# Softmax weights transposed by VectorE blocks and a round trip through DRAM instead of by TensorE

## The chip, the core and the metric

One core of one Trainium2 chip runs the whole program. The metric is device time in microseconds (us) of one execution. Five engines work side by side, each through its own instruction stream in order: PE (TensorE matmuls), DVE (VectorE), ACT (ScalarE), POOL (GpSimd) and SP (SyncE). POOL, SP and ACT also issue DMAs; an instruction that waits holds back what stands behind it on its engine. PEld is the loading of PE's weights, which runs beside the matmuls.

## What is computed

Two decoder layers on x of 512 rows by 1024 columns, all in float32. Layer 0 mixes tokens by dilated window attention, layer 1 by a gated linear recurrence (RG-LRU); after each comes a gated convolution FFN, and every sub-layer has a norm before and after it. Only the attention matters here. It has 24 heads of width 128 in three groups of 8, whose outputs are combined head by head with softmax denominators as weights:

```python
WINDOWS, DILATIONS = (128, 512, 2048), (1, 4, 16)
...
logits = einsum('bxhnqd,bxhnkd->bxhnqk', qs, kk) * scale + bias
logits = where(mask, logits, NEG_INF)
p = exp(logits - max(logits)); s = sum(p)
o = einsum('bxhnqk,bxhnkd->bxhnqd', p, vv) / s
...
alpha = softmax(stack(lses), axis=0)
o = sum(alpha[..., None] * stack(outs), axis=0)
```

The last product needs p with the keys on the partitions, while the softmax leaves it with the queries there. So every 128x128 block of p is transposed between the two products.

## The kernel before

**Large products.** Every weight matrix is loaded in pieces (`load`, L193, SP queue, three `raw` buffers), split into a high and a low float32r half (`split` L148 and `split_normed` L139: ACT makes `whi`, DVE makes `wlo`), and multiplied in three passes (`mm3`, L253, matmuls at L255; the value products at L643 and L702). At most eight split units wait in front of PE (`W_UNITS`).

**Order of work.** The program is written out by hand in one order. `feat_tiles` (L409) makes one output tile of 24 matmuls and calls `tick` (L222); `values` (L689) also ticks after each tile of 24 matmuls. A tick advances every side generator in `sides` whose delay has run out, and then `pump` (L167) converts one or two more weight units. A generator says with `yield n` after how many ticks it goes on. One tick is thus 24 matmuls of 512 columns.

**Local heads** (window 128, dilation 1). `local` (L744) runs once for each of 8 heads, two for each `hp`, one tick apart. Its first step loads a Toeplitz bias tile (`toeplitz`, L612, a DMA on POOL's queue), makes the scores on PE (L753, plain float32), adds the bias on DVE (L740) and takes the exponential on ACT (L766). Two ticks later it transposes the 7 blocks on PE (L775, into two PSUM banks), copied out by DVE (L780) and ACT (L778). One more tick later come the output products (L788) and their copy (L790).

**Strided heads** (dilations 4 and 16). `strided` (L793) takes the two groups of one head together, for 8 heads: Toeplitz tiles, scores (L803), bias (L740), exponentials (L818), normalising (L830). Two ticks later 8 transposes on PE (L837) and two copies on ACT (L839); then a row of coefficients goes through DRAM and comes back on all partitions (`crow` L842 and `cn` L844, POOL queue). Four ticks later (five for head 6) the output products (L850) and the combination on DVE (L853, L854).

**Blocks by DVE.** `turned` (L285) and `fetched` (L295) are already used by `prenorm` (L305) for one row tile of each of three norms: DVE turns each 32x32 block in itself (L288), one POOL DMA writes the tile to DRAM (L292), and four POOL DMAs of 32 partitions fetch it with the blocks in their places (L299). The tile that comes back is read through a strided view: 128 columns of one block are four runs of 32.

**Small vectors.** `feature_columns` (L524), a part of the generator `build`, loads biases and convolution weights as rows by POOL DMAs (L514), turns them on PE (L517) and copies them (L519); `ffn` and `lru` read them later.

**Buffers.** Nearly all 128x512 tiles come from one pool with 28 slots (`gen`, L118); a tile that takes a used slot waits for that slot's last reader. Toeplitz tiles have 2 slots, PSUM has 8 banks.

## Time and profile before

| | |
|---|---|
| Time, median of 3 runs | 1471.40 us (1471.37 to 1471.43) |
| The profiled execution's own time | 1471.48 us |
| Its span, first to last instruction | 1469.7 us |
| Granted TensorE clock | 0.998 |
| Busy share of PE, PEld, DVE, ACT, POOL | 99%, 84%, 58%, 46%, 4% |
| Transposes on PE at L775 and L837 | 56 and 64 |
| First score product of a local head, last output product of a strided one | 59.9 us, 481.9 us |

The profiled execution took 1471.48 us, of which 1.8 us lie outside its span. A PE row's duration is modelled and overlaps that of the next row, since matmuls are pipelined: what a matmul costs is read from the distance between starts.

### The profile page before, as it was taken

What the parts mean: (1) busy time and instruction counts of PE and PEld (TensorE: products, weight loads), DVE (VectorE), ACT (ScalarE), POOL (GpSimd) and SP (SyncE); (2) the same over time, 40 slices, a digit from 0 to 9 for tenths busy, and PEclk for the clock granted to TensorE, in tenths of its full rate; (3) what the DMA queues carried; (4) which work ended last, traced back from release to release, by engine and by line L of the source; (5) the groups of instructions that cost most, each with busy time, mean ns of one, the idle gap of its engine ahead of it and who ended that gap; (6) DMA issues with size and microseconds to landing.
All of it is one profiled execution on the core that took longest, in us unless ns stands there. A gap on an engine that the chain in (4) does not pass through costs nothing.

```text
span 1469.7 us, 18639 instructions
## 1 busy us (share of the span) xinstructions
PE 1461.2 (99%) x7006; PEld 1228.7 (84%) x7006; DVE 851.0 (58%) x1894; ACT 682.0 (46%) x1538; POOL 60.1 (4%) x141
## 2 busy tenths in 40 slices
PE   9999999999999999999999999999999999999998
PEld 7888888888888898888888888988898888888886
DVE  5645545454645786555564338868785555565333
ACT  7645536263625454433444234489554333444321
POOL 0500001010100100000000001000100000000000
PEclk9999999999999999999999999999999999999999
DMA  6622235343534433223233222441433223223201
GB/s 203 198 66 89 91 91 138 114 137 109 141 111 123 159 115 115 86 89 112 86 101 129 86 92 79 123 137 58 136 107 109 95 86 115 87 89 129 98 1 58
DMA packets 117331, 157.55 MB, mean 107 GB/s; under 512 B 5688, under 2 KB 98072, under 8 KB 117240
## 3 DMA queue, kind: packets, MB, share of 16 engines
q1 hardware_dynamic: 112104, 144.72, 30.1%
q0 software_dynamic: 4544, 10.58, 3.3%
q8 instruction: 55, 0.90, 0.3%
q10 hardware_dynamic: 592, 1.05, 0.2%
q14 instruction: 36, 0.29, 0.1%
HBM read 148.38 MB, written 7.95 MB: 106 GB/s over the span
## 4 chain that ended last, share of the span: by engine, by line
PE 93%; ACT 4%; DVE 3%; issue 0%; DVEq 0%; ACTq 0%
PE ps L255 55%; PE acc L255 24%; PE v L702 7%; PE v L643 2%; DVE xb L908 1%; PE O L850 1%; PE S L803 1%; PE O L788 1%; PE S L753 1%; DVE wlo L150 1%; ACT sig L929 1%; ACT whi L149 1%; PE tr L331 1%; PE PT L837 0%; PE PT L775 0%
## 5 line engine op out<-in xcount | busy, mean ns | idle before, releaser
L255 PE MATMUL ps<-hT,whi 128*128 128x512 f32 (+1 forms) x2752 | 801.8, 375 | 0.0
L255 PEld LDWEIGHTS ps<-hT,whi 128*128 128x128 f32 x2752 | 503.0, 188 | 91.4
L255 PE MATMUL ps<-hT,wlo 128*128 128x512 f32 (+1 forms) x1376 | 515.2, 374 | 0.0
L150 DVE TENSOR_TENSOR wlo<-raw,whi 128x512 fp32r<-128x512 f32 x360 | 230.9, 687 | 189.3 <-ACT whi L149 189.3
L255 PEld LDWEIGHTS ps<-hT,wlo 128*128 128x128 f32 x1376 | 259.0, 188 | 46.3
L149 ACT ACTIVATE whi<-raw 128x512 fp32r<-128x512 f32 x360 | 204.9, 623 | 135.2 <-PE acc L255 120.8
L567 DVE SCALAR_TENSOR_TENSOR u<-ps,cols,u 128x511 f32<-128x511 f32 x192 | 143.8, 749 | 140.6 <-ACT u L563 137.2
L255 PE MATMUL acc<-whi,ahi 128*128 128x512 f32 x512 | 199.6, 390 | 0.0
L255 PE MATMUL acc<-whi,alo 128*128 128x512 f32 x512 | 199.3, 389 | 0.2 <-DVE alo L150 0.2
L255 PE MATMUL acc<-wlo,ahi 128*128 128x512 f32 x512 | 199.2, 389 | 0.0
L143 ACT ACTIVATE whi<-raw,first_w 128x128 fp32r<-128x128 f32 (+1 forms) x432 | 147.2, 431 | 62.6 <-PE ps L255 52.9
L563 ACT ACTIVATE u<-ps,cols 128x512 f32<-128x512 f32 x96 | 75.0, 781 | 209.7 <-PE ps L255 209.7
L144 DVE SCALAR_TENSOR_TENSOR wlo<-raw,first_w,whi 128x128 fp32r<-128x128 f32 (+1 forms) x432 | 142.3, 394 | 37.4 <-ACT whi L143 37.3
L255 PEld LDWEIGHTS acc<-whi,alo 128*128 128x128 f32 x512 | 96.1, 188 | 20.6 <-DVE alo L150 0.6
L255 PEld LDWEIGHTS acc<-whi,ahi 128*128 128x128 f32 x512 | 96.1, 188 | 19.8
L255 PEld LDWEIGHTS acc<-wlo,ahi 128*128 128x128 f32 x512 | 96.1, 188 | 19.7
L702 PE MATMUL v<-whi,hT 128*128 128x512 f32 x320 | 103.6, 395 | 0.0
L702 PEld LDWEIGHTS v<-whi,hT 128*128 128x128 f32 x320 | 60.1, 188 | 12.1
L578 ACT ACTIVATE u<-u 128x512 f32<-128x512 f32 x48 | 30.4, 634 | 80.4 <-DVE u L567 80.4
L702 PE MATMUL v<-wlo,hT 128*128 128x512 f32 x160 | 62.3, 390 | 0.0
L382 DVE TENSOR_TENSOR post<-acc,gain 128x512 f32<-128x512 f32 x32 | 22.0, 687 | 45.3 <-ACT junk L262 45.3
L630 DVE TENSOR_TENSOR qk<-ps,roots 128x512 f32<-128x512 f32 x24 | 16.6, 691 | 53.3 <-PE ps L255 53.3
(168 smaller groups left out, 986.9 us busy)
## 6 DMA issues: line engine op xcount, KB each, us to landing
raw<-in_ffn_w_up_dram SPq DMA_DIRECT2D x48, 1024.0 KB, 5.2
raw<-in_attn_w_qkv_dram SPq DMA_DIRECT2D x26, 1024.0 KB, 5.1
raw<-in_ffn_w_down_dram SPq DMA_DIRECT2D x24, 1024.0 KB, 5.0
raw<-in_attn_w_qkv_dram SPq DMA_DIRECT2D x19, 512.0 KB, 6.3
raw<-in_lru_w_in_dram SPq DMA_DIRECT2D x8, 1024.0 KB, 5.4
vrows<-v SPq DMA_DIRECT2D x16, 256.0 KB, 3.8
vp<-vrows SPq DMA_DIRECT2D x16, 256.0 KB, 3.4
raw<-in_attn_w_o_dram SPq DMA_DIRECT2D x4, 1024.0 KB, 4.9
```

Of the source, the lines that this page charges most:

```text
L143: nc.scalar.activation(hi[:, k], raw[:, k], AF.Copy, scale=w)
L144: nc.vector.scalar_tensor_tensor(lo[:, k], raw[:, k], w, hi[:, k].bitcast(F32), op0=ALU.mult, op1=ALU.subtract)
L149: nc.scalar.activation(hi, raw, AF.Copy)
L150: nc.vector.tensor_tensor(lo, raw, hi.bitcast(F32), op=ALU.subtract)
L255: mm(dst, l[a], r[b], start=start and n == 0, stop=stop and n == 2)
L382: nc.vector.tensor_tensor(u[i], parts[i], g[:, at[i]], op=ALU.mult)
L563: nc.scalar.activation(u, ps, AF.Identity, scale=cc[:, j : j + 1], bias=cc[:, 48 + j : 49 + j])
L567: nc.vector.scalar_tensor_tensor(u[:, d:], ps[:, : S - d], wc, u[:, d:], op0=ALU.mult, op1=ALU.add)
L578: nc.scalar.activation(u, u, AF.Gelu_apprx_tanh)
L630: nc.vector.tensor_tensor(dst, src, row, op=ALU.mult)
L643: mm(banks[t], hT[a][:, k, t * P : (t + 1) * P], W[b][:, k % 2, :], start=u == n == 0, stop=u == 3 and n == 5,)
L702: mm(banks[t], hT[a][:, k, t * P : (t + 1) * P], W[b][:, k % 2, :], start=(k, a, b) == (0, 0, 0), stop=(k, a, b) == (KD - 1, 1, 0),)
```

## The change

Four things change.

- **Local heads**: all 8 turn p by `turned` and `fetched` in the first step, right behind the exponentials: a tile of 3 blocks and one of 4. The generator then yields 4 ticks where it yielded 2 and 1.
- **Strided heads**: heads 0 to 6 do the same behind the normalising, two tiles of 4 blocks, and yield 6 ticks (7 for head 6) where they yielded 2 and 4 (5). Head 7 keeps the transposes on PE. The DMA `crow` stands between the writes and the fetches, `cn` behind them.
- **Toeplitz tiles** are fetched one head ahead (`table`), and a strided head's two tiles lie in one buffer.
- **Rows of the small vectors** are loaded on the sync queue, in steps of the generator of their own (`column_rows`); their transposes follow in later steps.

The output products read the fetched tiles through the strided view. No head's arithmetic changes.

```diff
-    def turned(src, i):
-        T = gen(s="T")
+    def turned(src, n=4):
+        T = gen(s="T")[:, : n * P]
         nc.vector.transpose(
             T.rearrange("p (c n j) -> p c n j", c=4, j=32), src.rearrange("p (n c j) -> p c n j", c=4, j=32)
         )
-        d = dp.tile([P, 512], F32, name=nm("turned"))
+        d = dp.tile([P, n * P], F32, name=nm("turned"))
         nc.gpsimd.dma_start(d, T)
         return d
...
-    def columns(parts):
-        n = sum(c for _, c in parts)
+    def column_rows(parts):
         st = gen(s="st")
         at = 0
         for src, c in parts:
-            nc.gpsimd.dma_start(st[at : at + c, :P], src)
+            nc.sync.dma_start(st[at : at + c, :P], src)
             at += c
+        return st, at
+    def columns(st, n):
...
+        def table(strided, h, take=True):
+            if (strided, h) not in tables:
+                T = gp.tile([P, 256], F32, tag="toe", name=nm("toe"), bufs=TOE_BUFS)
+                for i in range(1 + strided):
+                    n = 256 >> strided
+                    toeplitz(T[:, i * n : i * n + n], i + strided, h, n)
+                tables[strided, h] = T
+            return tables.pop((strided, h)) if take else None
...
         def local(h, hh, q, k, v):
-            T = gp.tile([P, 256], F32, tag="toe", name=nm("toe"), bufs=TOE_BUFS)
-            toeplitz(T, 0, h, 256)
+            T = table(0, h)
...
-            yield 2
+            table(*((0, h + 1) if h < 7 else (1, 0)), False)
+            ds = [turned(L[0][:, P:], 3), turned(L[1])]
             blocks = [(a, j) for a in range(4) for j in range(2) if a or j]
-            pts = {}
-            for c in range(2):
-                grp = blocks[4 * c : 4 * c + 4]
-                ps = psum("PT")
-                for n, (a, j) in enumerate(grp):
-                    o = (a % 2) * 256 + j * P
-                    nc.tensor.transpose(ps[:, n * P : (n + 1) * P], L[a // 2][:, o : o + P], ident)
...
-            yield 1
+            pts = [fetched(ds[0], 3), fetched(ds[1])]
+            pts = {b: pts[n > 2][:, n - 3 * (n > 2)] for n, b in enumerate(blocks)}
+            yield 4
             po = psum("O")
...
-            yield 2
-            pts = []
-            for L in Ls:
-                ps = psum("PT")
-                for r in range(4):
-                    c = slice(r * P, (r + 1) * P)
-                    nc.tensor.transpose(ps[:, c], L[:, c], ident)
-                pt = gen(s="PT")
-                nc.scalar.activation(pt, ps, AF.Copy)
-                pts.append(pt)
+            if h < 7:
+                table(1, h + 1, False)
+                ds = [turned(L) for L in Ls]
             row = dp.tile([P, 4], F32, name=f"crow{h}")
             nc.gpsimd.dma_start(row, c0)
+            if h < 7:
+                pts = [fetched(d) for d in ds]
             cn = gen(s="cn")
             nc.gpsimd.dma_start(cn, bass.AP(tensor=row.tensor, offset=row.offset, ap=[[0, P], [1, S]]))
-            yield 5 if h == 6 else 4
+            if h < 7:
+                yield 7 if h == 6 else 6
+            else:
...
-                    mm(po[:, c], vtile(v, r, 2 * gi + hh), pts[gi][:, c], start=gi == 0, stop=gi == 1)
+                    mm(po[:, c], vtile(v, r, 2 * gi + hh), pts[gi][:, r], start=gi == 0, stop=gi == 1)
```

More of the change, by code (lines that the diff above doesn't have):

```diff
@@ L290, in turned, with fetched @@
         )
-        d = dp.tile([P, 512], F32, name=nm("turned"))
+        d = dp.tile([P, n * P], F32, name=nm("turned"))
         nc.gpsimd.dma_start(d, T)
         return d
-    def fetched(d):
-        t = gen(s="ft")
+    def fetched(d, n=4):
+        t = gen(s="ft")[:, : n * P]
         for c in range(4):
@@ L318, in prenorm @@
             return
-        ds = [turned(h, i) for i, h in enumerate(xs)]
+        ds = [turned(h) for h in xs]
         xt = [fetched(d) for d in ds]
@@ L526, in feature_columns @@
         v2 = lambda r: r.rearrange("n (j p) -> (n j) p", p=P)
-        cl = columns(
-            [(v(lru_conv_w[0, k]), 8) for k in range(4)]
-            + [(v(lru_conv_b[0]), 8), (v2(lru_ga_b[0]), 8), (v2(lru_gx_b[0]), 8), (v(lru_lambda[0]), 8)]
-        )
+        rows = [
+            column_rows(
+                [(v(lru_conv_w[0, k]), 8) for k in range(4)]
+                + [(v(lru_conv_b[0]), 8), (v2(lru_ga_b[0]), 8), (v2(lru_gx_b[0]), 8), (v(lru_lambda[0]), 8)]
+            )
+        ]
+        yield 1
+        for layer in range(2):
+            cw, cb = ffn_conv_w[layer], ffn_conv_b[layer]
+            rows.append(column_rows([(v(cw[0]), 48), (v(cw[1]), 48)]))
+            rows.append(column_rows([(v(cw[2]), 48), (v(cb), 48)]))
+            yield 1
+        cl = columns(*rows[0])
         lam = cl[:, 56:64]
@@ L550, in feature_columns @@
         for layer in range(2):
-            cw, cb = ffn_conv_w[layer], ffn_conv_b[layer]
-            ca = columns([(v(cw[0]), 48), (v(cw[1]), 48)])
-            cc = columns([(v(cw[2]), 48), (v(cb), 48)])
-            ffn_cols[layer] = (ca, cc)
+            ffn_cols[layer] = tuple(columns(*rows[1 + 2 * layer + i]) for i in range(2))
             yield 1
@@ L615, in toeplitz @@
             nc.gpsimd.dma_start(dst, bass.AP(tensor=rowv[g].tensor, offset=o, ap=[[1, P], [1, n]]))
+        tables = {}
+        def table(strided, h, take=True):
[6 more added lines that the diff above has]
+            return tables.pop((strided, h)) if take else None
         vrows = []
@@ L766, in local @@
                 nc.scalar.activation(ls, ls, AF.Exp, bias=neg[:, a : a + 1], accum_out=st0[:, a, 1, h : h + 1])
-            yield 2
+            table(*((0, h + 1) if h < 7 else (1, 0)), False)
+            ds = [turned(L[0][:, P:], 3), turned(L[1])]
             blocks = [(a, j) for a in range(4) for j in range(2) if a or j]
-            pts = {}
-            for c in range(2):
-                grp = blocks[4 * c : 4 * c + 4]
-                ps = psum("PT")
-                for n, (a, j) in enumerate(grp):
-                    o = (a % 2) * 256 + j * P
-                    nc.tensor.transpose(ps[:, n * P : (n + 1) * P], L[a // 2][:, o : o + P], ident)
-                pt = gen(s="PT")
-                if c:
-                    nc.scalar.activation(pt[:, : len(grp) * P], ps[:, : len(grp) * P], AF.Copy)
-                else:
-                    nc.vector.tensor_copy(pt, ps)
-                for n, b in enumerate(grp):
-                    pts[b] = pt[:, n * P : (n + 1) * P]
-            yield 1
+            pts = [fetched(ds[0], 3), fetched(ds[1])]
+            pts = {b: pts[n > 2][:, n - 3 * (n > 2)] for n, b in enumerate(blocks)}
+            yield 4
             po = psum("O")
@@ L796, in strided @@
             Ls = []
+            T = table(1, h)
             for gi, (q, k) in enumerate(qks):
-                T = gp.tile([P, 256], F32, tag="toe", name=nm("toe"), bufs=TOE_BUFS)
-                toeplitz(T[:, :P], gi + 1, h, P)
                 ps = psum("S")
@@ L806, in strided @@
                     c = slice(r * P, (r + 1) * P)
-                    scores(L[:, c], ps[:, c], T[:, :P], mx[:, 4 * gi + r : 4 * gi + r + 1])
+                    scores(L[:, c], ps[:, c], T[:, gi * P : gi * P + P], mx[:, 4 * gi + r : 4 * gi + r + 1])
                 Ls.append(L)
@@ L830, in strided @@
                 nc.vector.tensor_tensor(L3, L3, rden.unsqueeze(2).to_broadcast([P, 4, P]), op=ALU.mult)
-            yield 2
-            pts = []
-            for L in Ls:
-                ps = psum("PT")
-                for r in range(4):
-                    c = slice(r * P, (r + 1) * P)
-                    nc.tensor.transpose(ps[:, c], L[:, c], ident)
-                pt = gen(s="PT")
-                nc.scalar.activation(pt, ps, AF.Copy)
-                pts.append(pt)
+            if h < 7:
+                table(1, h + 1, False)
+                ds = [turned(L) for L in Ls]
             row = dp.tile([P, 4], F32, name=f"crow{h}")
             nc.gpsimd.dma_start(row, c0)
+            if h < 7:
+                pts = [fetched(d) for d in ds]
             cn = gen(s="cn")
             nc.gpsimd.dma_start(cn, bass.AP(tensor=row.tensor, offset=row.offset, ap=[[0, P], [1, S]]))
-            yield 5 if h == 6 else 4
+            if h < 7:
+                yield 7 if h == 6 else 6
+            else:
+                yield 2
+                pts = []
+                for L in Ls:
+                    ps = psum("PT")
+                    for r in range(4):
+                        c = slice(r * P, (r + 1) * P)
+                        nc.tensor.transpose(ps[:, c], L[:, c], ident)
+                    pt = gen(s="PT")
+                    nc.scalar.activation(pt, ps, AF.Copy)
+                    pts.append(pt.rearrange("p (r c) -> p r c", r=4))
+                yield 4
             po = psum("O")
```

## The prediction, made before the changed kernel had run

> **What bounds the kernel now.** First the page: the span, the engines, the chain that ended last. Then the waits of PE, and the two attention stages as windows (busy us and count of each engine, clock, DMA share).

> ```profile
> span 1469.7 us, 18639 instructions
> PE 1461.2 (99%) x7006; PEld 1228.7 (84%) x7006; DVE 851.0 (58%) x1894; ACT 682.0 (46%) x1538; POOL 60.1 (4%) x141
> PE 93%; ACT 4%; DVE 3%; issue 0%; DVEq 0%; ACTq 0%
> ```
> ```profile
> PE warm L1024 <- DVE one L1056: 1.5, 1, 1.5
> PE v L643 <- ACT hT L345: 0.2, 1, 0.2
> PE acc L255 <- DVE alo L150: 0.2, 1, 0.2
> ```
> ```profile
> 59.00:215.00 156.00, 156.00 (x784) 132.18 (x783) 85.67 (x290) 79.26 (x248) 5.64 (x10) 1.00 0.30 93
> 215.00:483.00 268.00, 268.00 (x1345) 227.26 (x1345) 142.12 (x480) 123.78 (x385) 16.15 (x30) 1.00 0.44 131
> ```

> PE carries 93% of the chain and waits 1.9 us in all, none of it in the attention. In the local stage (59 to 215) and the strided one (215 to 483) it never rests, at full clock; DVE is busy 55% and 53%, POOL 4% and 6%. So a matmul that goes shortens the span by its cost, unless something else comes late; work given to DVE, POOL or the DMA engines is free while its result is in time.

> **What goes from PE.** The rows of transposes, and their neighbourhood in time:

> ```profile
> L837 PE MATMUL PT<-ident,L 128*128 128x128 f32 x64 | 8.3, 272 | 0.0
> L775 PE MATMUL PT<-ident,L 128*128 128x128 f32 x56 | 7.5, 273 | 0.0
> ```
> ```profile
> 185.33 0.39 PE L255 MATMUL ps<-hT,wlo 128*128 128x512 f32 x1
> 185.56 0.93 PE L775 MATMUL PT<-ident,L 128*128 128x128 f32 x7
> 186.24 0.70 PE L255 MATMUL ps<-hT,whi 128*128 128x512 f32 x2
> 186.79 0.40 PE L255 MATMUL ps<-hT,wlo 128*128 128x512 f32 x1
> ...
> 237.01 0.39 PE L702 MATMUL v<-wlo,hT 128*128 128x512 f32 x1
> 237.24 0.39 PE L702 MATMUL v<-whi,hT 128*128 128x512 f32 x1
> 237.47 1.03 PE L837 MATMUL PT<-ident,L 128*128 128x128 f32 x8
> 238.26 0.48 PE L702 MATMUL v<-whi,hT 128*128 128x512 f32 x1
> 238.57 0.39 PE L702 MATMUL v<-wlo,hT 128*128 128x512 f32 x1
> ```

> A 512-column matmul costs 0.23 us (237.01 to 237.24), so a tick of 24 is 5.45 us. From 237.24 to 238.57 there are two such steps and one group of 8 transposes: 1.33 - 0.45 = 0.88 us. From 185.33 to 186.79 there are three steps and a group of 7: 1.46 - 0.68 = 0.78 us. Removed are 7 strided groups (head 7 keeps its own) and 8 local ones: 7 x 0.88 + 8 x 0.78 = 6.2 + 6.2 = **12.4 us**.

> [...]

> **What is added, and whether it comes in time.** The prices are those of the norm's tile, which goes the same way at 497 us:

> ```profile
> L780 DVE COPY PT<-PT 128x512 f32<-128x512 f32 x8 | 5.5, 688 | 15.1 <-PE PT L775 15.1
> L288 DVE STREAM_TRANSPOSE T<-xs 128x512 f32<-128x512 f32 x6 | 3.9, 688 | 0.0
> L292 POOL DMA_DIRECT2D turned<-T x6 | 3.3, 550 | 530.8 <-DVE T L288 530.7
> L299 POOL DMA_DIRECT2D ft<-turned x24 | 13.3, 562 | 5.5 <-DMA turned<-T 5.4
> ```
> ```profile
> 497.77 1.14 POOL L292 DMA_DIRECT2D turned<-T  x2 [31.16 <-DVE T L288]
> 500.71 4.38 POOL L299 DMA_DIRECT2D ft<-turned  x8 [1.80 <-DMA turned<-T]
> ```
> ```profile
> 509.78 0.63 ACT L324 ACTIVATE hT<-ft 128x512 fp32r<-128x512 f32 x1 [1.43 <-DMA ft<-turned]
> ```

> Two writes, a wait of 1.80 us for them, eight fetches: from the first write's issue to the first use of the second tile 509.78 - 497.77 = 12.0 us, beside weight loads. Now a local head:

> ```profile
> 171.57 1.68 PE L753 MATMUL S<-qk,qk 128*128 128x128 f32 x8
> 176.10 0.19 ACT L766 ACTIVATION_READ_ACCUMULATOR L<-L,s 128x1 f32 x1
> 176.61 2.41 DVE L144 SCALAR_TENSOR_TENSOR wlo<-raw,first_w,whi 128x128 fp32r<-128x128 f32 x8 [2.27 <-ACT whi L143]
> 178.55 0.38 PE L753 MATMUL S<-qk,qk 128*128 128x128 f32 x2
> ```

> Scores start at 171.57 and the exponentials end at 176.29, 4.7 us on. A second block turn of 0.69 us follows (the first falls into DVE's idle time before 176.61); taking the 12.0 us from there, the tiles are there 17.4 us after the scores began. The output products come four ticks later, 4 x 5.45 = 21.8, plus 1.3 us of the scores themselves: 23.1 at the least. The next head starts 7.0 us later, while POOL needs 11 DMAs x 0.55 + 1.8 = 7.9 a head: 0.9 less for the second. **Slack 5 us or more.** A strided head:

> ```profile
> 230.23 1.95 PE L803 MATMUL S<-qk,qk 128*128 128x128 f32 x16
> 231.93 0.48 PE L702 MATMUL v<-whi,hT 128*128 128x512 f32 x1
> ```
> ```profile
> 240.04 1.29 DVE L830 TENSOR_TENSOR L<-L,s 128x512 f32<-128x512 f32 x2
> ```

> The second of a pair is worst: normalised 11.1 us after its scores began, 1.3 later because of the first head's two turns, two turns of its own (1.3), the 12.0, and `crow` in between (0.55): 26.3 us. Six ticks give 32.7. Slack 6 us, and `cn`, issued last, still fits if it lands like a fetch. Head 7's `crow` now stands behind head 6's fetches, which by the same sum are over 26.3 us after head 6's scores, about 19 after its own: 13 us before its use.

> Behind the waiting instructions: on POOL, behind a `turned` that waits for DVE, stand only the same head's fetches and later heads' DMAs. The Toeplitz tile of the next head stands ahead of it, so it is earlier than now. On DVE, the turn waits for ACT's exponentials, and behind it stand weight splits (L144): 0.7 us later for each local head, 1.3 for a strided one, less the 0.69 of each L780 copy that goes. Whether splits can be late:

> ```profile
> ACT whi L143 <- PE ps L255: 52.9, 13, 6.0
> ```
> ```profile
> SPq L199 <- DVE wlo L144: 322.0, 35, 20.5
> ```

> ACT waits 52.9 us for PE to give back unit buffers and PE never for a split: up to eight units, one a tick, stand ready. Cost nothing; without that cover it would be about 15 us. ACT loses its 22 copies.

> The rows of the small vectors: 16 DMAs more on SP, in two steps of the generator with eight and eight. SP's loads wait 322 us for splits, so SP is mostly idle; even at POOL's 0.55 us apiece they hold it for 9 us in all, and a load so delayed still has the eight-tick lead of its units, 43 us. Nothing. Each set's transposes stand three ticks (16 us) behind its DMAs; from POOL they landed within 4.9 us, which with the issue makes 14 us at the worst:

> ```profile
> DMA to landing us min/median/max: 1.9/3.9/4.9
> ```

> The output products wait on eight DMA semaphores where there were one or two. The nearest row is the small vectors' transposes:

> ```profile
> L517 PEldq EVENT_SEMAPHORE  x8: 51/51/51, 70.1 to 84.9; - x8
> L517 PEld LDWEIGHTS cols<-ident,st x5: 135/139/143, 74.2 to 88.8; 96*128 96x128 f32 x4, 64*128 64x128 f32 x1
> ```

> PE's sequencer passed those waits at 70.1, 4 us before their matmul ran at 74.2. So waits are hidden: between 0 and 15 heads x 4 x 0.05 = 3 us; I take 0.2, near the row.

> Last, the products read four runs of 32 columns instead of one of 128. No PE row does that. ACT reads the same view:

> ```profile
> L324 ACT ACTIVATE hT<-ft 128x512 fp32r<-128x512 f32 x6 | 3.8, 632 | 3.8 <-DMA ft<-turned 3.8
> L149 ACT ACTIVATE ahi<-u 128x512 fp32r<-128x512 f32 x48 | 28.7, 617 | 0.0
> ```

> 632 against 617 ns. And a float32 pass of 128 columns takes 0.11 us (16 from 230.23 to 231.93), twice the time per column of the float32r passes (0.23 for 512): PE takes these columns at half the rate that it can. Bounds 0 and a halved rate, 224 passes x 0.11 = 25 us; nothing below zero, as no matmul goes. I take 0, by the ACT rows.

> **Sum.** 1471.48 - 12.4 + 0.2 = 1459.3; the profiled execution lies 0.08 above the median, hence **1459.2 us**.

> **Rivals.**
> 1. *POOL's queue is late* (slower). Let a DMA take POOL p us. From the first head's scores of a local pair, the second head's last tile is there after 4.7 (exponentials) + 21 p (DMAs of both heads) + 2.4 (waits for writes) + 4.7 (last issue to use, 505.09 to 509.78) = 11.8 + 21 p; PE wants it after 7.0 + 23.1 = 30.1. It decides from p = 0.87; at 1.02 each of four pairs is 3.1 us late and the gain is gone; at 1.3 it is 9 us a pair, 1459 + 36 = 1495. For it: 11 DMAs a head where there was one. Against: every group of POOL's DMA issues that I saw has means near the 0.55 and 0.56 above, beside a DVE that is half busy. 4%.
>    [...] 1%.
> 2. *The strided operand costs PE.* Decides at 0.055 us a pass; at the bound 1459 + 25 = 1484. 5%.
> 3. *Durations, not distances, are the price*: 1471.5 - 112 x 0.272 = 1441. Against it: the starts. 2%.
> 4. *The freed time turns into waiting*, for splits or fetches in part: 1463 to 1471. Against: the slacks above. 5%, of which 3% within 0.2% of before.

> **How the numbers follow.** The forecast has 83%: 1459.2. Without any cost of waits it is 1459.0; a misreading of 0.1 us in each of the 15 groups is 1.5 either way, and the waits can cost 3: 1457.5 to 1463.5, which is the range. The rivals hold the other 17% and lie mostly outside. A measurement tells 0.2% (2.9 us) from no change. Faster: 83, rival 3 with 2, the milder part of rival 4 with 2 and of rival 2 (under 0.04 us a pass) with 2: 0.89. Same: 3 of rival 4: 0.03. Slower: 5 of rival 1 and 3 of rival 2: 0.08.

> **What would show it.** Right: PE still without waits at the output products; the L299 fetches landing before PE reaches them; groups of 16 output passes still 1.7 us long; span 1457.5. Wrong: a row of PE waiting for ft, or POOL issues above 1 us (rival 1); output groups longer at unchanged count (rival 2); PE waiting for wlo or whi (rival 4). A price that I took as zero without a row, the strided read on PE, is the weakest step.

## The result, and the profile after

The changed kernel takes 1459.15 us (median of 4 runs, 1458.85 to 1459.46), the kernel before 1471.41 us (4 runs, 1471.37 to 1471.57): ratio 0.9916, 95% interval 0.9899 to 0.9934. The profiled execution of the changed kernel took 1459.46 us.

The first rows of its page, its chain and all of PE's waits (us in total, times, longest):

```profile
span 1457.7 us, 18749 instructions
PE 1448.4 (99%) x6894; PEld 1217.2 (84%) x6894; DVE 862.4 (59%) x1916; ACT 669.5 (46%) x1516; POOL 134.4 (9%) x275
PE 92%; ACT 4%; DVE 3%; issue 1%; DMA 0%; POOL 0%; DVEq 0%; ACTq 0%
```
```profile
PE warm L1040 <- DVE one L1072: 1.5, 1, 1.5
PE v L664 <- ACT whi L143: 0.4, 1, 0.4
PE O L866 <- DMA ft<-turned: 0.3, 1, 0.3
PE v L664 <- ACT hT L345: 0.2, 1, 0.2
```

PE has 112 matmuls fewer and is busy 12.8 us less; the span is 12.0 us shorter, and PE still rests for only 2.4 us. POOL's busy time went from 60 to 134 us and DVE's rose by 11 us; neither shows in the span. One wait of 0.3 us is new in kind: an output product that waits for a fetch. The 0.4 us for a split (`whi`) lies at 6.5 us, ahead of the attention.

The two attention stages as windows (columns as in the prediction), the strided one cut at 471 us, where its last head now ends:

```profile
59.00:215.00 156.00, 156.00 (x756) 131.44 (x755) 90.31 (x304) 74.30 (x239) 50.95 (x92) 1.00 0.48 144
215.00:471.00 256.00, 255.75 (x1261) 216.41 (x1260) 147.58 (x484) 116.55 (x371) 53.41 (x98) 1.00 0.54 161
```

PE is full in both, at full clock. The strided stage is 12 us shorter by the clock on the wall because the local stage's gain has moved it forward too. The DMA engines' mean share rose from 0.30 to 0.48 and from 0.44 to 0.54. The groups of the added work and of the output products (busy us, mean ns of one, idle before):

```profile
L299 POOL DMA_DIRECT2D ft<-turned x144 | 79.0, 556 | 42.8 <-issue 17.2 <-DMA turned<-T 12.5 <-ACT whi L143 11.9
L292 POOL DMA_DIRECT2D turned<-T x36 | 19.6, 547 | 761.0 <-DVE T L288 756.2 <-DVE wlo L144 3.9 <-DMA ft<-turned 0.4
L866 PE MATMUL O<-ft,vp 128*128 128x128 f32 x112 | 13.9, 275 | 0.3 <-DMA ft<-turned 0.3
L866 PE MATMUL O<-PT,vp 128*128 128x128 f32 x16 | 1.9, 275 | 0.0
```

A POOL issue costs 0.55 us as before. The two L866 rows stand side by side in one kernel: passes that read the strided view (`ft`) and head 7's, which read contiguous columns (`PT`), both 275 ns. These durations are modelled, but the starts agree: a group of 16 of either kind lasts 1.95 us, as before, so its passes start equally far apart (0.11 us):

```profile
466.55 1.95 PE L866 MATMUL O<-ft,vp 128*128 128x128 f32 x16
468.34 1.95 PE L866 MATMUL O<-PT,vp 128*128 128x128 f32 x16
```

The cover for the splits held, though ACT's wait for PE to give back units fell from 52.9 us:

```profile
ACT whi L143 <- PE ps L255: 33.5, 9, 6.4
```

**How much in time the fetches are.** From the landings of the DMAs in the trace: the last fetch of a head landed so long before the first matmul that reads it (us). At strided head 1 that matmul had itself been held up 0.25 us for the fetch.

| head | 0 | 1 | 2 | 3 | 4 | 5 | 6 | 7 |
|---|---|---|---|---|---|---|---|---|
| local | 10.1 | 7.2 | 12.7 | 11.3 | 10.0 | 9.4 | 11.2 | 9.4 |
| strided | 14.8 | 0.1 | 14.0 | 3.9 | 14.9 | 4.3 | 9.6 | - |

The local heads and the first strided head of each pair have more than was worked out (5 and 6 us or more); the second strided heads have less, and head 1 has nothing.

### The profile page after: what moved, and what is told of

Its sections match the earlier page's. It is cut to its first block, busy times and chain, and to the rows that moved or that the text cites. A ratio compares the mean times of both kernels' runs of the same rounds, so it can differ in the third digit from the quotient of the medians.

```text
span 1457.7 us, 18749 instructions
## 1 busy us (share of the span) xinstructions
PE 1448.4 (99%) x6894; PEld 1217.2 (84%) x6894; DVE 862.4 (59%) x1916; ACT 669.5 (46%) x1516; POOL 134.4 (9%) x275
## 4 chain that ended last, share of the span: by engine, by line
PE 92%; ACT 4%; DVE 3%; issue 1%; DMA 0%; POOL 0%; DVEq 0%; ACTq 0%
PE ps L255 54%; PE acc L255 24%; PE v L723 7%; PE v L664 1%; DVE xb L924 1%; PE S L811 1%; PE O L797 1%; PE O L866 1%; PE S L773 1%; DVE wlo L150 1%; ACT sig L945 1%; ACT whi L149 1%; PE tr L331 1%; DMA ft<-turned 0%; ACT sig L964 0%
## 5 line engine op out<-in xcount | busy, mean ns | idle before, releaser
L255 PE MATMUL ps<-hT,whi 128*128 128x512 f32 (+1 forms) x2752 | 801.4, 375 | 0.0
L255 PEld LDWEIGHTS ps<-hT,whi 128*128 128x128 f32 x2752 | 503.7, 188 | 91.5
L255 PE MATMUL ps<-hT,wlo 128*128 128x512 f32 (+1 forms) x1376 | 515.4, 375 | 0.0
L150 DVE TENSOR_TENSOR wlo<-raw,whi 128x512 fp32r<-128x512 f32 x360 | 230.8, 686 | 187.7 <-ACT whi L149 187.7
L255 PEld LDWEIGHTS ps<-hT,wlo 128*128 128x128 f32 x1376 | 259.1, 188 | 46.5
L149 ACT ACTIVATE whi<-raw 128x512 fp32r<-128x512 f32 x360 | 204.6, 621 | 135.3 <-PE acc L255 120.9
L255 PE MATMUL acc<-whi,ahi 128*128 128x512 f32 x512 | 199.7, 390 | 0.0
L255 PE MATMUL acc<-whi,alo 128*128 128x512 f32 x512 | 199.4, 389 | 0.1
L255 PE MATMUL acc<-wlo,ahi 128*128 128x512 f32 x512 | 199.3, 389 | 0.0
L143 ACT ACTIVATE whi<-raw,first_w 128x128 fp32r<-128x128 f32 (+1 forms) x432 | 145.9, 425 | 57.3 <-PE ps L255 33.5
L144 DVE SCALAR_TENSOR_TENSOR wlo<-raw,first_w,whi 128x128 fp32r<-128x128 f32 (+1 forms) x432 | 140.3, 390 | 9.3 <-ACT whi L143 9.3
L255 PEld LDWEIGHTS acc<-whi,alo 128*128 128x128 f32 x512 | 96.1, 188 | 20.4 <-DVE alo L150 0.5
L255 PEld LDWEIGHTS acc<-whi,ahi 128*128 128x128 f32 x512 | 96.2, 188 | 19.8
L255 PEld LDWEIGHTS acc<-wlo,ahi 128*128 128x128 f32 x512 | 96.2, 188 | 19.8
L292 POOL DMA_DIRECT2D turned<-T x36 | 19.6, 547 | 761.0 <-DVE T L288 756.2
L299 POOL DMA_DIRECT2D ft<-turned x144 | 79.0, 556 | 42.8 <-issue 17.2
L723 PEld LDWEIGHTS v<-whi,hT 128*128 128x128 f32 x320 | 60.1, 188 | 12.2
```

What stands on the lines that cost most here:

```text
L143: nc.scalar.activation(hi[:, k], raw[:, k], AF.Copy, scale=w)
L144: nc.vector.scalar_tensor_tensor(lo[:, k], raw[:, k], w, hi[:, k].bitcast(F32), op0=ALU.mult, op1=ALU.subtract)
L149: nc.scalar.activation(hi, raw, AF.Copy)
L150: nc.vector.tensor_tensor(lo, raw, hi.bitcast(F32), op=ALU.subtract)
L255: mm(dst, l[a], r[b], start=start and n == 0, stop=stop and n == 2)
L292: nc.gpsimd.dma_start(d, T)
```

## The experiments

The times of before in these runs were 1471.40 to 1471.42. Each edit starts from the changed kernel unless said otherwise.

**1. Only the local heads by VectorE and DRAM.**

```
 if h < 7:
     table(1, h + 1, False)
-    ds = [turned(L) for L in Ls]
...
-if h < 7:
-    yield 7 if h == 6 else 6
-else:
-    yield 2
+yield 2
+# head 7's transposes and copies, for every head
+yield 5 if h == 6 else 4
```

> Changed kernel with the strided heads turned on TensorE as before; only the eight local heads go by VectorE and DRAM. Theory (PE's passes at the distance of their starts are the whole gain, 0.78 us a local group of 7): 1459.15 + 7 x 0.88 = 1465.3, no wait of PE on a fetch. Rival 'durations are the price and the added way pays part of it back': 64 of the 120 passes would not give half of the gain in this way; 56 x 0.272 = 15 us gross, and the time would lie away from 1465 by what the local heads' way costs (below 1462 or above 1468).

Measured: 1465.26 us (1465.23 to 1465.37), ratio 0.9958 [0.9943, 0.9973]; no wait of PE on a fetch. That is the theory's number.

**2. Only the strided heads.**

```
-ds = [turned(L[0][:, P:], 3), turned(L[1])]
-pts = [fetched(ds[0], 3), fetched(ds[1])]
-yield 4
+yield 2
+# the transposes and copies of the kernel before
+yield 1
```

> Changed kernel with the local heads turned on TensorE as before; only strided heads 0 to 6 go by VectorE and DRAM. Theory: 1459.15 + 8 x 0.78 = 1465.4, plus at most the one wait of 0.3 us that the changed kernel has on a strided fetch. Rival 'the strided heads pay their way' (their second tile has almost no slack in the trace of the changed kernel): above 1466.

Measured: 1466.20 us (1466.11 to 1466.66), ratio 0.9965 [0.9952, 0.9978]: 0.8 above the theory's sum. By its number the rival was right, but not by its cause. PE's wait in this kernel:

```profile
PE O L878 <- DMA vp<-vrows: 0.6, 1, 0.6
```

The fetches had at least 4.2 us to spare here. What came late was the other input of the same products: the values, which go through DRAM too (`vrows` out, `vp` back, both on SP). They had not been in the prediction at all. Together the two halves give 6.15 + 5.21 = 11.4 us, the whole 12.3.

**3. No transposes, nothing in their place.** The copies out of PSUM go too, and the output products read the weights unturned, so this kernel does not compute the layer. Edit of the kernel before:

```
-    nc.tensor.transpose(ps[:, n * P : (n + 1) * P], L[a // 2][:, o : o + P], ident)
...
+pts = {(a, j): L[a // 2][:, (a % 2) * 256 + j * P :][:, :P] for a, j in blocks}
...
-    nc.tensor.transpose(ps[:, c], L[:, c], ident)
...
+pts = Ls
```

> Kernel before with all transposes of the softmax weights and their copies out of PSUM left out and nothing put in their place (the output products read the weights unturned, head 7 included): the gross price of the passes alone. Theory: 1471.41 - 8 x 0.78 - 8 x 0.88 = 1458.1, so that the changed kernel (1459.15, which keeps head 7's group of 0.88) pays 0.2 us at most for all that it adds. Rival 'durations are the price': 120 x 0.272 = 33 us less, 1438.8, and the change pays 20 us for its way.

Measured: 1458.01 us (1457.94 to 1458.06), ratio 0.9909 [0.9894, 0.9924]: 13.4 us for 16 groups, where the working gives 13.3. With head 7's group put back (0.88), a change that cost nothing would stand at 1458.9. The changed kernel pays 0.26 us for all that it adds, which is less than its own runs differ (0.6).

**4. The old transposes back on PE, read by nobody.**

```
-yield 4
+yield 2
+# 7 transposes of L into two PSUM tiles
+yield 2
...
-    yield 7 if h == 6 else 6
+    yield 2
+    # 8 transposes of Ls into two PSUM tiles
+    yield 5 if h == 6 else 4
```

> Changed kernel with the old groups of transposes put back on TensorE beside the new way, at their old distance after the scores (two ticks), their results read by nobody. Local output products stand four ticks after the scores as in the changed kernel. Theory (only PE's passes count; the copies that left ACT and DVE count nothing): 1459.15 + 12.4 = 1471.5, within 0.5. Rival 'part of the gain comes from the copies leaving ACT and DVE': as much below 1471 as that part is; all of it would leave 1459.

Measured: 1472.35 us (1472.20 to 1473.32), ratio 1.0008 [0.9998, 1.0017]. All of the gain is gone; the copies that left ACT and DVE show no worth of their own. It lies 0.85 above the sum; about 0.7 of that is already there at the first strided head (its scores start at 223.70 where the kernel before starts them at 222.99, from the same start of the first local head). It is no listed wait, but most of it lies in one group, the third local head's, right behind transposes of the small vectors: its 7 passes hold PE from 104.32 to 105.59, 1.27 us, where the same group of the kernel before takes 0.68 (104.52 to 105.20).

```profile
104.32 1.21 PE L797 MATMUL PT<-ident,L 128*128 128x128 f32 x7
105.59 0.50 PE L723 MATMUL v<-whi,hT 128*128 128x512 f32 x1
```

Why that group is longer stays open.

**5. Strided products one tick earlier.**

```
-yield 7 if h == 6 else 6
+yield 6 if h == 6 else 5
```

> Changed kernel with the output products of strided heads 0 to 6 one tick (5.45 us) earlier. Slack as the prediction worked it out (6 us for every second head): nothing is late, 1459.2. Slack as read from the landings in the trace of the changed kernel (last fetch to first output product: 0.1, 3.9 and 4.3 us for heads 1, 3 and 5; 9.6 and more for the others): 5.3 + 1.5 + 1.1 = 7.9 us of waits, about 1467, all of them at those three heads.

Measured: 1469.92 us (1468.19 to 1474.56), ratio 0.9992 [0.9983, 1.0001]. One tick takes nearly the whole gain. PE's waits, and the clock around the second of them (columns as above; PEclk is the third from the end):

```profile
PE O L866 <- DMA vp<-vrows: 5.1, 4, 2.4
PE O L866 <- DMA ft<-turned: 1.6, 2, 1.4
```
```profile
256.00:258.00 2.00, 1.05 (x5) 0.55 (x3) 0.69 (x1) 1.13 (x2) 1.03 (x2) 1.00 0.54 130
258.00:260.00 2.00, 1.33 (x8) 1.20 (x9) 0.00 (x0) 0.20 (x1) 0.63 (x2) 0.90 0.82 168
260.00:262.00 2.00, 2.00 (x11) 2.00 (x11) 0.69 (x1) 0.00 (x0) 0.00 (x0) 0.50 0.18 27
262.00:264.00 2.00, 2.00 (x9) 1.58 (x8) 1.93 (x3) 0.00 (x0) 0.00 (x0) 0.75 0.00 0
```

Both theories missed. Most of the waiting is for `vp`, not for the fetches, and it moves the fetches' use so far that only head 1's are still late. And waiting costs more than its length: PE's waits at these products grew by 6.4 us (0.3 to 6.7), its busy time by 4.5 (1448.4 to 1452.9, the same 6894 matmuls). After the wait at 258 us the granted clock stood at 0.50 for 3.41 us, which by my estimate makes 1.7 of the 4.5. Part of the rest is waiting that the record counts as busy: head 2's 16 passes start over 3.26 us, where 1.67 is usual and 0.86 are listed waits.

**6. Local products two ticks earlier.**

```
-yield 4
+yield 2
```

> Changed kernel with the local heads' output products two ticks (10.9 us) earlier. Prediction's slack (5 us or more at every head): up to 5.9 us late in each of four pairs and a little more in the second heads, about 24 us, 1483. Landings in the trace of the changed kernel (slack 7.2 to 12.7, head by head): late by 0.8, 2.9, 0, 0, 0.9, 0.6, 0, 1.5, together 6.7, about 1466.

Measured: 1483.62 us (1481.93 to 1484.38), ratio 1.0081 [1.0068, 1.0095]. The number is that of the prediction's slack, and it is right by accident. The waits, and the stretch after the longest:

```profile
PE O L797 <- DMA ft<-turned: 14.0, 4, 4.7
PE O L797 <- DMA toe<-rowv: 1.2, 2, 0.9
```
```profile
87.39 2.05 PE L797 MATMUL O<-ft,v 128*128 128x128 f32 x8 [4.71 <-DMA ft<-turned]
...
90.08 1.05 PE L723 MATMUL v<-whi,hT 128*128 128x512 f32 x2
90.94 0.63 PE L723 MATMUL v<-wlo,hT 128*128 128x512 f32 x1
...
94.05 0.62 PE L723 MATMUL v<-whi,hT 128*128 128x512 f32 x2
94.50 0.39 PE L723 MATMUL v<-wlo,hT 128*128 128x512 f32 x1
```
```profile
82.45:85.87 3.42, 0.22 (x3) 0.03 (x1) 0.34 (x1) 0.00 (x0) 0.00 (x0) 1.00 1.12 310
85.87:89.28 3.41, 1.89 (x9) 1.93 (x10) 0.00 (x0) 0.00 (x0) 0.00 (x0) 0.50 0.23 54
89.28:92.69 3.41, 3.41 (x10) 2.64 (x10) 2.30 (x8) 2.93 (x9) 0.00 (x0) 0.50 0.00 0
92.69:96.11 3.42, 3.42 (x17) 2.82 (x16) 0.10 (x1) 0.00 (x0) 0.00 (x0) 1.00 0.00 0
```

PE waited 15 us, 11.7 of them in the second heads of the pairs (4.7, 0.2, 2.7 and 4.0), where the landings had put 5.0 of 6.7: since PE moves and the fetches of one head hold the next one's, landings of another order could not be carried over. The other 10 us are its own busy time (1448.4 to 1458.5). After a wait of 4.7 us the matmuls stand 0.43 us apart (two from 90.08 to 90.94), and 0.225 again at 94: the granted clock was 0.50 from 85.87 to 92.69, and three times more for 3.41 us. In these stretches PE was busy for 14.8 us; at half clock that makes an estimated 7.4 of the 10 us. PE had not rested all through before each fall: in the 3.41 us before the four of them it rested 3.2, 2.7, 2.0 and 3.4 us, and before the one in experiment 5 it rested 1.6 (last section).

**7. The small vectors' rows back on POOL's queue.**

```
-nc.sync.dma_start(st[at : at + c, :P], src)
+nc.gpsimd.dma_start(st[at : at + c, :P], src)
```

> Changed kernel with the sixteen DMAs of the small vectors' rows back on POOL's queue; their transposes stay where the change put them (93.7 us on). Theory (that part of the change is worth nothing): they go out behind local head 1's fetches, from 82.4 us, 8.8 us of issues, and land ahead of 93.7: 1459.2, within 0.4. Rival 'they had to leave POOL': head 2's writes (91.3 us) and the small transposes late, PE waiting for st or ft, 3 us or more, above 1462.

Measured: 1461.04 us (1460.08 to 1461.67), ratio 0.9927 [0.9913, 0.9940]. The ratios' intervals overlap with the changed kernel's; the times do not (its slowest is 1459.46), so the moved rows seem worth 1 to 2 us, where I had nothing. The rival's way was wrong as well: head 2's first write goes out at 91.2 us, as with the rows on SP (91.3), and no small transpose waits. PE's new waits lie far from the rows:

```profile
PE tr L331 <- DVE xs L314: 1.4, 1, 1.4
PE O L866 <- DMA vp<-vrows: 0.9, 1, 0.9
```

One is the values' way again, in the last pair at 468 us, the other a norm's tile at 910 us, behind fetches that started at 887.6 where the changed kernel's start at 884.4. Why either should follow from rows loaded at 85 us I cannot say.

**8. Bias tables not fetched ahead.**

```
-table(*((0, h + 1) if h < 7 else (1, 0)), False)
...
-table(1, h + 1, False)
```

> Changed kernel with the bias tables not fetched one head ahead, but at the head's own start. Theory (POOL's queue holds a head's DMAs behind the fetches and the small row of the head ahead of it): the second head of a pair gets its table some 10 us later than its scores can run, more in the strided pairs; worked out from the landings, about 10, 6 and 7 us late at strided heads 1, 3, 5 and 4 to 5 in the local pairs together: about 1487. Rival (the slack of 5 to 6 us covers it, the tables matter nothing): 1459 to 1461.

Measured: 1499.70 us (1497.37 to 1501.83), ratio 1.0192 [1.0178, 1.0206]: slower than the kernel before. POOL and DVE around the second local head:

```profile
67.31 4.37 POOL L299 DMA_DIRECT2D ft<-turned  x8 [0.79 <-DMA turned<-T]
72.93 0.56 POOL L624 DMA_DIRECT2D toe<-rowv  x1 [1.24 <-DMA ft<-turned]
```
```profile
76.27 0.29 DVE L761 CUSTOM_DVE_ANT_0 L<-S,toe 128x128 f32<-128x128 f32 x1 [8.14 <-DMA toe<-rowv]
```

The table, behind the first head's fetches, comes 8.1 us after DVE could score. Right in kind, 13 us too small: the largest wait is one that I had not listed. Head 7's own transposes on PE, whose tables also come late, wait 13.1 us for its weights.

**9. Head 7 too.**

```
-if h < 7:
-    ds = [turned(L) for L in Ls]
+ds = [turned(L) for L in Ls]
...
-    # head 7: yield 2, transposes on PE, yield 4
+yield 7 if h == 6 else 6
```

> Changed kernel with head 7 too turned by VectorE and placed by DRAM, its output products at their old place. Theory: PE gains 0.9 us, and the last tile lands late: the writes go out behind head 6's cn (456.7 us) and the fetches land 12 to 13 us later, 468.7 to 470, where PE wants them at 467.4: 1.3 to 2.6 us of wait, 1459.5 to 1461. Rival (the six ticks that were enough for the others are enough here): 1458.3.

Measured: 1467.71 us (1466.71 to 1470.13), ratio 0.9977 [0.9969, 0.9986]. The direction is the theory's, the size is not:

```profile
465.16 1.95 PE L852 MATMUL O<-ft,vp 128*128 128x128 f32 x16
471.37 0.46 PE L852 MATMUL O<-ft,vp 128*128 128x128 f32 x2 [4.26 <-DMA ft<-turned]
473.89 3.33 PE L852 MATMUL O<-ft,vp 128*128 128x128 f32 x14 [2.07 <-DMA ft<-turned]
```
```profile
470.00:474.00 4.00, 0.57 (x3) 0.44 (x3) 0.00 (x0) 0.00 (x0) 0.57 (x1) 0.74 1.04 302
474.00:478.00 4.00, 4.00 (x17) 3.81 (x18) 1.28 (x2) 0.00 (x0) 0.00 (x0) 0.50 0.79 270
```

Head 7's products follow straight on head 6's. The writes went out at 456.5, as expected, but the last fetch landed at 473.8, not at 470. The DMA share is 1.04 (the next stage's weights come in); that this is the reason is read off, not tested. The clock then fell to 0.50. The six ticks of the others would not do here, which is why this head keeps its transposes on PE.

**10. Strided products of heads 0 to 5 one tick later.**

```
-yield 7 if h == 6 else 6
+yield 7
```

> Changed kernel with the output products of strided heads 0 to 5 one tick later. Theory: the one wait on a fetch (0.3 us at head 1, whose last fetch lands 0.1 us ahead of its use) goes, nothing else: 1458.9, and no wait of PE at line 866. Rival (buffers kept longer stall something): above 1459.5.

Measured: 1459.00 us (1458.98 to 1459.03), ratio 0.9916 [0.9902, 0.9929]. No wait for `ft` or `vp` is left:

```profile
PE warm L1040 <- DVE one L1072: 1.5, 1, 1.5
PE v L664 <- ACT hT L345: 0.2, 1, 0.2
```

0.15 us below the changed kernel's median, inside its spread; it is the fastest version that computes everything, if only by that.

**11. crow and cn from ScalarE's queue.**

```
-nc.gpsimd.dma_start(row, c0)
+nc.scalar.dma_start(row, c0)
...
-nc.gpsimd.dma_start(cn, ...)
+nc.scalar.dma_start(cn, ...)
```

> Changed kernel with crow and cn issued from ScalarE's queue. Theory (POOL's queue, where cn waits for crow's landing, holds the second head's writes): writes of heads 1, 3, 5 go out up to 3 us earlier (head 1: 237.5 to 238 where they went at 240.9), the wait of 0.3 us at head 1 goes: 1458.9. ScalarE waits 2.5 to 4 us eight times for crow to land; the eight units of split weights hide that. Rival (ScalarE's waits come through): splits late, PE waiting for whi, above 1460.

Measured: 1461.24 us (1459.88 to 1464.35), ratio 0.9931 [0.9917, 0.9945]; the profiled execution is the longest of the five. Half of the theory holds: the second heads' slack rises from 0.1, 3.9 and 4.3 us to 3.8, 9.1 and 8.4. But head 1's writes went out only 0.7 us earlier (240.48 for 241.15), not 3. POOL around them:

```profile
236.97 0.56 POOL L624 DMA_DIRECT2D toe<-rowv  x1 [0.96 <-DMA ft<-turned]
239.92 0.57 POOL L624 DMA_DIRECT2D toe<-rowv  x1 [2.39 <-issue]
240.48 1.08 POOL L292 DMA_DIRECT2D turned<-T  x2
```

A table's fetch reads nothing of a fetch's, and still waits for one to land (0.96 us). In the traces of the kernel before and of the changed kernel, POOL's DMAs (98 and 232) bear eight semaphores in turn, and none goes out before the DMA eight ahead of it has landed; the nearest follow that landing by 0.28 us. So landings held the queue too: with eight DMAs in flight it stood still, and in the changed kernel the tables wait 10.1 us in this way.

```profile
POOL toe L624 <- DMA ft<-turned: 10.1, 8, 2.6
```

But that is not what kept head 1's writes. The DMA eight before the second table's had landed at 236.9, and this table went out at 239.92, after 2.39 us that the profile puts down to no wait (`issue`); without them the writes would have gone at 238.1, as the theory has it. The changed kernel has the same before head 0's `cn`, whose last wait in the record ended at 236.8:

```profile
239.51 0.57 POOL L847 DMA_DIRECT2D cn<-crow  x1 [5.09 <-issue]
```

What holds POOL there stays open. Most of what head 1 gained came behind its writes: the first landed 4.2 us after its issue, where it took 7.8. And ScalarE's wait does come through, at a place that neither theory had named:

```profile
453.86 0.33 ACTq L843 DMA_DIRECT2D crow<-s  x1
458.25 0.33 ACTq L847 DMA_DIRECT2D cn<-crow  x1
```
```profile
PE acc L255 <- ACT ahi L149: 2.3, 1, 2.3
```

For the last head ACT stands still until `crow` has landed, and behind it are the splits of the attention's output, which PE needs at once.

**12. Both together.**

```
 # the edits of 9 and of 11
```

> The two before this together: all heads go by VectorE and DRAM, crow and cn on ScalarE's queue. Theory: head 7's writes go out at about 456 us, after head 6's fetches begin to land, and its tile lands 0 to 1.6 us late: 1458.0 to 1459.7. Rival (PE has nothing between head 6's and head 7's products, so any lateness of vp or ft shows): as the run with head 7 alone, 1459.5 to 1461.

Measured: 1466.26 us (1464.10 to 1467.43), ratio 0.9963 [0.9951, 0.9976]; both missed. Head 7's tile now lands 4.0 us ahead of its use, so the price of experiment 9 was lateness and not the way itself. What PE waits for is ACT again, and the norm's tiles, as in experiment 7:

```profile
PE tr L331 <- DVE xs L314: 3.2, 2, 2.4
PE acc L255 <- ACT ahi L149: 2.0, 1, 2.0
```

These sum to 5.2 us of 7.1 over the changed kernel; what holds up the norm's tiles stays open here too.

## Why the prediction was right

1. **PE bounds; a transpose costs the distance of starts: right, shown.** 12.4 us were worked out for 15 groups; leaving 16 groups out takes 13.4 (experiment 3), the local eight alone are worth 6.15 for 6.2 (1), and putting them back takes the gain away (4). The third rival's 1441 is excluded by experiment 3's 1458.0.
2. **Turns, writes and fetches are hidden: right in sum, 0.26 us** (3), 0.1 with one tick more (10), both within the runs' spread. DVE's turns, ACT's lost copies and the splits behind them have no visible cost.
3. **Local slack "5 us or more": right,** 7.2 to 12.7.
4. **Strided slack 6 us for the second of a pair: wrong, 0.1, 3.9 and 4.3.** The failed step is the chain "11.1 us after its scores began, 1.3 later ..., two turns of its own (1.3), the 12.0, and `crow` in between (0.55): 26.3 us". It took 36.8 us at head 1 (223.96 to 260.74), 32.6 and 32.2 at heads 3 and 5. Its first part held: head 1's turns ended at 237.4, 13.4 us after its scores began, for 13.7. Two things were left out. First POOL's queue: head 0's `cn` stood ahead of head 1's writes until 239.51, partly for landings and partly for a reason that the trace does not show (11), and the writes went out at 241.15, 3.7 us after the turns. Then the DMA engines: the 12.0 came from the norm's stage, and here it took 19.6 from the first write's issue to the last landing. That write alone took 7.8 us to land, where the norm's first took 2.3; beside it ran head 0's `cn`, the values on their way back and weight loads, with a DMA share of 0.99 from 241 to 249. That these are the reason is read off the trace, not tested. The gain was saved by the demand side: PE came to these products 36.3 us after the scores, not 32.7, since head 1's scores and head 0's output products (1.7 us each) lie in between. That the two errors cancelled to within 0.25 us at head 1 is luck; one tick less costs 10.8 us (5).
5. **Rival 1 (POOL's queue late): not so** at 0.556 us an issue. But its form, issues alone, was wrong: landings held the queue too (10.1 us of waits of the tables), and so did stretches that the trace puts down to no wait (2.39 and 5.09 us) (11). No run shows a ground for the second chance there, 1%: POOL's issues took 0.547 and 0.556 us (L292 and L299) in the changed kernel.
6. **The strided operand at 0, the "weakest step": right, shown** by the two L866 groups of equal length, and by the 0.26 us in all (3): over 224 such passes that leaves 0.001 us each.
7. **Semaphore waits 0.2: not visible.** The count was right: 63 such waits at the output products (32 at L797, 31 at L866, 51 ns each) where the kernel before has 4. But of the 0.26 in all, 0.25 is head 1's one wait for a fetch, and with that gone 0.1 is left for everything (10). The bound of 3 us is excluded.
8. **The small vectors' rows: nothing was taken.** 1.9 us when undone (7), by a way that I do not know; open.
9. **The tables fetched ahead** were passed over in one sentence ("earlier than now"). They are a condition of the gain: 40.6 us without them (8).
10. **Not seen at all:** `vp`, the other input of the strided products, due nearly as soon as the fetches (2, 5).

## What to carry to other kernels

Here a pass that left the bounding engine was worth the distance between starts (13.3 us worked out, 13.4 measured in experiment 3), so long as what replaced it was in time; work that out for every input of the consumer, from latencies of the same stage, with the queue's other waits and what is in flight in it. In these runs a late input cost its wait and then more: half clock behind the waits made an estimated 1.7 us in experiment 5 and 7.4 in experiment 6. On an in-order queue, put ahead what the next step needs first: here the tables, 40.6 us (experiment 8).
